# Row masks for the parts of eight running streams, and gate sums from token quarters

## The chip, the cores and the metric

The kernel runs on one core of a Trainium2 chip. The metric is the device time of one execution in microseconds (us). The core's engines are PE (TensorE, matrix products into PSUM), DVE (VectorE), ACT (ScalarE), POOL (GpSimd) and SP (which only starts DMAs here). Each engine takes its instructions in its own fixed order.

## The reference, cut to what matters

Two layers are applied to one prompt of 1024 tokens and to 8 running streams of 16 tokens each. The second layer, mixer B, is an mLSTM with 4 heads of width 512; only its two places below are changed.

```
gates = concat([q, k, v]) @ w_gates + b_gates          # 8 columns: 4 input gates, 4 forget gates
num   = (s @ v) + w_inter * (q @ C)                    # per token of a stream; C is 512x512
C_new = decay * C + k^T (w * v)                        # per head and per stream
h     = num / max(|den|, exp(-m_t))
```

For the running streams, `C` comes from outside: 4 heads x 8 streams = 32 matrices of 1 MB, each of which is read, multiplied by 16 queries (`q @ C`), updated and written back.

## The kernel before, in words

Tokens are held as 9 tiles of 128 (8 of the prompt, the ninth holds the 8 streams of 16), or as three thirds of 384. Activations lie with features on the partitions.

**Features.** Mixer B's input part runs over 16 blocks of 128 features (`Feature`). At the end of each, `gates` (L819) adds the block's share of the gates of all 1152 tokens into one PSUM tile `gp` (L721): one matmul for each third, weights `gsum` of 8 columns, each into its own column tile of TensorE (partitions 0, 32, 64). After the last block three copies (L905) bring `gp` to SBUF.

**z steps and streams.** Then 24 steps compute the z half of the projection (`z_to`), and the main loop runs over 32 units (head h, tile n of 128 prompt tokens). The 32 `Stream`s, in order of head and then of stream b = 0..7, ride in both: `open_stream` loads C into two tiles `c0`, `products` (L1130) is called one step or unit later, `finish` (L1152) after it. Streams 0 to 9 ride in the z steps, streams 10 to 31 with one unit each. I number them s0 to s31; each head has eight, so s7, s15, s23 and s31 are the last of their heads (b = 7).

`products` makes `q @ C` for 32 tokens, of which 16 belong to this stream: four matmuls `sm<-c,qT` of 32 columns, one for each quarter of the 512 features, side by side in the four column tiles; the four 32-row parts of the PSUM tile `pa` still have to be added. ACT copies `pa` to a tile `ev` (L1141). Then four matmuls on `sk` and four DVE operations (`c<-c,decB,sm`, L1148) update C.

`finish` does something when b is 3 or 7. A quad of four matmuls `sm<-ev,selm` adds the parts of four streams and puts the 16 useful rows of each into 32 rows of `po`; ACT copies the result and starts a store to `ni_d`. `rows_out` (L1324) reads it back when the unit of the ninth tile (a rider) is computed.

Other names in the rows: `x` (L1399) adds a projection to the residual, `raw<-sm,colB,sk` (L1380) is the skip gate, `dd` (L1230) the decay mask, which needs the loaded row `cw`, `bst` and `dn` (L1337, L1343) the head norm, `Cst` (L1297) the prompt's matrix memory, `Ch`/`Cl`, `va`, `s`, `q` the high and low parts of operands of three-pass products.

**What sets the order.** PE's order is the program's order (all its instructions pass through `Ordered`, so they all show L58). The order on the other engines is set when the kernel is built, by a scheduler that works with its own estimate of when each operand is ready; on the chip each engine keeps that order and waits where an operand is late. PSUM is eight buffers, all named `sm`, given out in rotation.

Of the kernel before, what the change touches and what calls it, by code (L numbers as in the profile page):

```python
# [8 lines left out]
F32 = mybir.dt.float32  # L9
F32R = mybir.dt.float32r  # L10
AF = mybir.ActivationFunctionType
# [59 lines left out]
def trunk_kernel(ctx: ExitStack, tc: tile.TileContext, ins: dict, outs: list):  # L71
# [57 lines left out]
    sk_d = [dram.tile([DH, NT * P], F32, name=f"sk_d{h}") for h in range(H)]  # L129
    z_d = [dram.tile([DH, NT * P], F32, name=f"z_d{h}") for h in range(H)]  # L130
    cw_d = dram.tile([H, 2, NT * P], F32, name="cw_d")
    ni_d = [dram.tile([2, P, DH], F32, name=f"ni_d{h}") for h in range(H)]
    x1_d = [dram.tile([P, D], F32, name=f"x1_d{n}") for n in range(NT)]
    st_d = [dram.tile([SB, 3 * SL, 2, DH], F32R, name=f"st_d{h}") for h in range(H)]

# [582 lines left out]
    gtok = const.tile([P, NT, 8], F32, name="gtok")  # L718
    G.memset(gtok, 0.0)

    gp = ps.tile([P, BT], F32, name="sm")  # L721
    cv0 = ins["state_mlstm_conv"][0].rearrange("b j e -> (b j) e")


    class Feature:
# [93 lines left out]
        def gates(self):  # L819

            f = self.f
            for b in range(NB):
                T.matmul(gp[32 * b:32 * b + 8], gsum[:, 0, f], self.xc[b], start=(f == 0), stop=(f == NF - 1), skip_group_check=True)

        def new_history(self):
            f = self.f
# [75 lines left out]
    gt = gt_stack.enter_context(tc.tile_pool(name="gt", bufs=1, side="right", reuse_waits="tile"))  # L902
    NTK = NT * P
    gsb = gt.tile([8, NTK], F32, name="rA")
    for b in range(NB):  # L905
        V.tensor_copy(out=gsb[:, b * BT:(b + 1) * BT], in_=gp[32 * b:32 * b + 8])
    z_to(4)


# [118 lines left out]
        T.transpose(tp[:, c * 32:(c + 1) * 32], n0t[:, c * P:(c + 1) * P], ident[:32, :32])  # L1028
    V.tensor_copy(out=n0T.rearrange("p c b h -> p (c b h)"), in_=tp[:, :P])

    selm = dw.tile([P, 2, 32], F32, name="selm")
    G.memset(selm, 0.0)
    for r0 in range(0, P, 32):
        for q in range(2):
            V.tensor_copy(out=selm[r0:r0 + 32, q, :SL], in_=ident[r0:r0 + 32, r0 + q * SL:r0 + (q + 1) * SL])

    def load_qkv(pool, h, n, want, prev=None, bufs=None):

# [80 lines left out]
    class Stream:  # L1119
# [12 lines left out]
        def products(self):  # L1132
            d, b = self.d, self.b
            pa = ps.tile([P, DH], F32, name="sm")

            b2 = slice(b // 2 * 32, b // 2 * 32 + 32)
            for c in range(DC):
                T.matmul(pa[32 * c:32 * c + 32], d.g["qT"][:, c, b2], self.c0[c // 2][:, c % 2], start=True, stop=True)
            ev = dw.tile([P, DH], F32, name="ev", bufs=4)
            d.ev.append(ev)  # L1140
            d.last = A.copy(out=ev, in_=pa)  # L1141
            for hf in range(2):
                c0 = self.c0[hf]
                for cc in range(2):
                    c = hf * 2 + cc
                    pc = ps.tile([P, DH], F32, name="sm")
                    T.matmul(pc, self.sk[:, 0, c * P:(c + 1) * P], self.sk[:, 1, :], start=True, stop=True)
                    V.scalar_tensor_tensor(out=c0[:, cc], in0=c0[:, cc], scalar=decB[:, d.h, 8 + b:9 + b], in1=pc,  # L1148
                                           op0=ALU.mult, op1=ALU.add)
                S.dma_start(out=C_s[0, b, d.h, hf * 256:(hf + 1) * 256].rearrange("(c p) e -> p c e", p=P), in_=c0)  # L1150

        def finish(self):  # L1152

            d, b = self.d, self.b
            if b % 4 == 3:
                po = ps.tile([P, DH], F32, name="sm")
                for i in range(4):
                    T.matmul(po[32 * i:32 * i + 32], selm[:, i % 2], d.ev[i], start=True, stop=True)
                d.ev = []
                ni = rawp.tile([P, DH], F32, name="raw")  # L1160
                A.copy(out=ni, in_=po)
                A.dma_start(out=ni_d[d.h][b // 4], in_=ni)

    heads = []
    streams = []
# [149 lines left out]
    def rows_out(u, a):  # L1315
# [5 lines left out]
        if u.smp:  # L1321
            if a == 0:
                u.ni = rawp.tile([P, DH], F32, name="raw")
                S.dma_start(out=u.ni, in_=ni_d[h].rearrange("a (b r) e -> (a b) r e", r=32)[:, :SL])  # L1324
            V.tensor_tensor(out=hn[:, a, :256], in0=num[:, :256], in1=u.ni[:, a * 256:(a + 1) * 256], op=ALU.add)
            if a == 0:
                V.tensor_tensor(out=hn[:, 0, 256:257], in0=num[:, 256:257], in1=dint[:, h:h + 1], op=ALU.add)
# [279 lines left out]
```

## Time and profile before

| what | value |
|---|---|
| time of the runs shown | 1933.91 us median of 3 (1932.88 to 1936.30) |
| profiled execution | 1929.5 us, span of the core 1927.8 us |
| granted TensorE clock | 0.996 |
| PE busy | 1887.7 us, 98% |
| DVE, ACT, POOL busy | 63%, 45%, 35% |
| features, from the first gate block to the last | 871.7 to 1138.0 us |
| quads `sm<-ev,selm` | 1272.8 to 1757.1 us |

The engine that sets the time is PE, so a change counts by what it does to PE: columns that it streams, gaps between two kinds of matmul, and waits. A timeline row groups instructions of one kind that follow each other; a record of a matmul includes its pipeline, so the next row can start before it ends. What a block costs is read from its start to the start of what follows it.

### The profile page before, as it was taken

Reading aid. Unit: us, or ns where it says so; the run is one execution under the profiler, and the core shown is the slowest. Engines: PE = TensorE matmul, PEld = TensorE weight load, DVE = VectorE, ACT = ScalarE, POOL = GpSimd, SP = SyncE. Lnnn points to the kernel's source line nnn. Section 1 sums busy time; section 2 is a strip of 40 time slices with the busy share of each in tenths; the row PEclk is TensorE's granted clock in tenths of the full one; section 3 lists DMA queues with packets and bytes.
Section 4 is the critical chain, followed back from the end, with each engine's and each line's share of the span. In section 5 each row is a group of like instructions: output and inputs, shape, how many; then the busy total and the mean of one; then the engine's idle time right before and its main releaser. Section 6 shows DMA issues by size and latency. Waiting matters only on the chain.

```text
span 1927.8 us, 32016 instructions
## 1 busy us (share of the span) xinstructions
PE 1887.7 (98%) x11553; PEld 1676.0 (87%) x11553; DVE 1216.1 (63%) x2406; ACT 862.4 (45%) x1760; POOL 674.9 (35%) x725
## 2 busy tenths in 40 slices
PE   7999999999999999999999999999999999999998
PEld 6888999999999778888999989888977887788887
DVE  5832567777776454567666655222388687688786
ACT  5422444444444343446655554222354444444564
POOL 2000234444442000024444421100167457457586
PEclk9999999999999999999999999999999999999999
DMA  6222343333334854435555564787898898876543
GB/s 217 93 93 73 96 109 100 100 98 99 101 97 122 263 152 143 131 92 157 152 160 166 164 186 124 240 256 247 263 320 267 263 287 273 262 239 196 153 130 125
DMA packets 345305, 328.20 MB, mean 170 GB/s; under 512 B 28164, under 2 KB 276436, under 8 KB 345148
## 3 DMA queue, kind: packets, MB, share of 16 engines
q1 hardware_dynamic: 278444, 255.72, 43.4%
q10 hardware_dynamic: 66512, 69.85, 11.7%
q8 instruction: 91, 1.49, 0.3%
q14 instruction: 66, 0.54, 0.1%
q0 software_dynamic: 192, 0.59, 0.1%
HBM read 203.07 MB, written 123.02 MB: 169 GB/s over the span
## 4 chain that ended last, share of the span: by engine, by line
PE 79%; DMA 7%; DVE 5%; POOL 3%; ACT 2%; issue 2%; ACTq 0%; SPq 0%; POOLq 0%; DVEq 0%
PE sm L58 79%; DMA cw<-cw_d 1%; POOL Cl L90 1%; DMA out<-c 1%; DMA z_d<-st 1%; DVE c L1148 1%; POOL va L90 1%; DMA kT<-k_d 1%; DMA vv<-vb_d 1%; DMA c<-in_state_mlstm_C 1%; DVE raw L1380 0%; DVE w L90 0%; DMA st_d<-w 0%; POOL q L90 0%; DVE Cst L1297 0%
## 5 line engine op out<-in xcount | busy, mean ns | idle before, releaser
L58 PE MATMUL sm<-xh,w 128*128 128x384 f32 x1536 | 410.4, 341 | 1.8 <-issue 1.2
L58 PEld LDWEIGHTS sm<-xh,w 128*128 128x128 f32 x1536 | 281.0, 188 | 10.0 <-issue 6.5
L58 PE MATMUL sm<-xl,w 128*128 128x384 f32 x768 | 260.1, 339 | 0.0
L58 PE MATMUL sm<-Xh,w 128*128 128x288 f32 x1024 | 216.9, 299 | 4.3 <-ACT c L499 4.3
L58 PE MATMUL sm<-w,o 128*128 128x512 f32 x864 | 209.7, 398 | 2.1 <-ACT o L89 1.2
L58 PE MATMUL sm<-w,os 128*128 128x512 f32 x864 | 200.3, 393 | 4.5 <-ACT os L89 3.5
L58 PEld LDWEIGHTS sm<-w,os 128*128 128x128 f32 x864 | 162.4, 189 | 40.8 <-ACT os L89 6.0
L58 PEld LDWEIGHTS sm<-w,o 128*128 128x128 f32 x864 | 160.0, 188 | 40.2 <-ACT o L89 1.4
L58 PE MATMUL sm<-w,Xh 128*128 128x512 f32 x576 | 180.5, 394 | 0.9 <-DVE w L90 0.9
L58 PEld LDWEIGHTS sm<-Xh,w 128*128 128x128 f32 x1024 | 168.9, 190 | 4.7 <-ACT c L499 4.5
L58 PE MATMUL sm<-S,w 128*128 128x288 f32 x1152 | 163.8, 297 | 0.0
L90 DVE TENSOR_TENSOR w<-r,w 128x512 fp32r<-128x512 f32 x176 | 137.9, 790 | 35.1 <-ACT w L89 34.4
L58 PEld LDWEIGHTS sm<-S,w 128*128 128x128 f32 x1152 | 155.1, 188 | 0.8
L90 POOL TENSOR_TENSOR Cl<-Cst,Ch 128x514 fp32r<-128x514 f32 x96 | 128.7, 1352 | 73.6 <-ACT Ch L89 50.3
L58 PE MATMUL sm<-Xl,w 128*128 128x288 f32 x512 | 151.9, 297 | 0.0
L58 PEld LDWEIGHTS sm<-xl,w 128*128 128x128 f32 x768 | 144.8, 189 | 0.0
L90 DVE TENSOR_TENSOR w<-raw,w 128x1024 fp32r<-128x1024 f32 x43 | 55.9, 1300 | 130.6 <-ACT w L89 126.6
L89 ACT CAST w<-r 128x512 fp32r<-128x512 f32 x176 | 107.2, 618 | 61.5 <-PE sm L58 29.1
L58 PEld LDWEIGHTS sm<-w,Xh 128*128 128x128 f32 x576 | 108.2, 190 | 24.0 <-DVE w L90 1.8
L58 PE MATMUL sm<-w,Xl 128*128 128x512 f32 x288 | 113.0, 392 | 0.0
L90 DVE TENSOR_TENSOR os<-or,os 128x384 fp32r<-128x384 f32 x96 | 52.8, 555 | 88.0 <-ACT os L89 87.8
L58 PE MATMUL sm<-va,k 128*128 128x258 f32 (+1 forms) x768 | 102.9, 284 | 0.5 <-DVE raw L1380 0.4
(310 smaller groups left out, 3643.5 us busy)
## 6 DMA issues: line engine op xcount, KB each, us to landing
c<-in_state_mlstm_C SPq DMA_DIRECT2D x64, 512.0 KB
out<-c SPq DMA_DIRECT2D x64, 512.0 KB
r<-in_a_w_in SPq DMA_DIRECT2D x96, 256.0 KB
or<-o_d SPq DMA_DIRECT2D x96, 192.0 KB
raw<-in_b_w_in SPq DMA_DIRECT2D x32, 512.0 KB
qT<-q_d SPq DMA_DIRECT2D x40, 256.0 KB
vh<-v_d SPq DMA_DIRECT2D x48, 192.0 KB
vb_d<-st ACTq DMA_DIRECT2D x48, 192.0 KB
```

Source lines behind the costliest of these rows:

```text
L58: ins = fn(*args, **kw)
L89: first = A.copy(out=hi, in_=src)
L90: (lo_eng or V).tensor_tensor(out=lo, in0=src, in1=f32(hi), op=ALU.subtract)
L1148: V.scalar_tensor_tensor(out=c0[:, cc], in0=c0[:, cc], scalar=decB[:, d.h, 8 + b:9 + b], in1=pc, op0=ALU.mult, op1=ALU.add)
```

## The change

Four edits.

1. `gates`: the 1152 tokens are put into four column tiles of 288 token columns each, in place of three of 384. As a block's `xc` still comes in thirds, the four quarters are made by six matmuls (288, 96, 192, 288, 192 and 96 columns). `gp` is cleared by DVE first, and four copies of 8x288 take it to SBUF.
2. `products`: two streams share one `ev` tile. Each stream's `pa` holds 32 rows for each quarter, of which alternate 16 rows are its own; the even stream's are kept by ACT with a scale of 1 or 0 for each row (`qsel[:, 0]`), the odd stream's are added by one DVE operation, `ev = pa * qsel[:, 1] + ev`.
3. `finish`: the quad is made only when b = 7, with the four shared tiles; `selm` is then a plain sum of the four quarters, and the result has all 128 rows of the head.
4. `ni_d` is one tile for each head, stored and read back in one piece; `selm` is made by 4 copies in place of 8, and `qsel` by one sum over `blk8`.

```
-    gp = ps.tile([P, BT], F32, name="sm")
+    gp = ps.tile([P, QT], F32, name="sm")
+    V.memset(gp, 0.0)
...
-            for b in range(NB):
-                T.matmul(gp[32 * b:32 * b + 8], gsum[:, 0, f], self.xc[b], start=(f == 0), stop=(f == NF - 1), skip_group_check=True)
+            for q, b, c0, c1, o in ((0, 0, 0, 288, 0), (1, 0, 288, 384, 0), (2, 1, 192, 384, 0), (3, 2, 96, 384, 0),
+                                    (1, 1, 0, 192, 96), (2, 2, 0, 96, 192)):
+                T.matmul(gp[32 * q:32 * q + 8, o:o + c1 - c0], gsum[:, 0, f], self.xc[b][:, c0:c1], start=(f == 0 and o == 0), stop=(f == NF - 1), skip_group_check=True)
...
+    selm = dw.tile([P, 32], F32, name="selm")
     for r0 in range(0, P, 32):
+        V.tensor_copy(out=selm[r0:r0 + 32], in_=ident[r0:r0 + 32, r0:r0 + 32])
+    qsel = dw.tile([P, 2], F32, name="qsel")
+    V.tensor_reduce(out=qsel, in_=blk8.rearrange("p (a q) -> p q a", q=2), axis=mybir.AxisListType.X, op=ALU.add)
...
-            ev = dw.tile([P, DH], F32, name="ev", bufs=4)
-            d.ev.append(ev)
-            d.last = A.copy(out=ev, in_=pa)
+            if b % 2 == 0:
+                ev = dw.tile([P, DH], F32, name="ev", bufs=4)
+                d.ev.append(ev)
+                d.last = A.activation(out=ev, in_=pa, func=AF.Copy, scale=qsel[:, 0:1])
+            else:
+                ev = d.ev[-1]
+                d.last = V.scalar_tensor_tensor(out=ev, in0=pa, scalar=qsel[:, 1:2], in1=ev, op0=ALU.mult, op1=ALU.add)
...
-            if b % 4 == 3:
+            if b == SB - 1:
                 po = ps.tile([P, DH], F32, name="sm")
                 for i in range(4):
-                    T.matmul(po[32 * i:32 * i + 32], selm[:, i % 2], d.ev[i], start=True, stop=True)
+                    T.matmul(po[32 * i:32 * i + 32], selm, d.ev[i], start=True, stop=True)
...
-                A.dma_start(out=ni_d[d.h][b // 4], in_=ni)
+                A.dma_start(out=ni_d[d.h], in_=ni)
```

On PE nothing but the gate blocks and the quads is different; of the eight quads those of s3, s11, s19 and s27 are gone. On DVE, 16 operations `ev<-sm,qsel,ev` are new. Where one of them stands is shown for s23, the last stream of the third head. DVE before, from the second half of the projection `x` of a unit to the update of C (c_16764 and c_16766 are the two tiles of C of s23):

```order
L1399 TENSOR_TENSOR x_3_14029<-x_3_14029,sm 128x512
L1230 TENSOR_TENSOR dd<-cw,m_pr 128x128
L1399 TENSOR_TENSOR x_3_14029<-x_3_14029,sm 128x512
L1380 SCALAR_TENSOR_TENSOR raw<-sm,colB,sk 128x128 x4
L1337 BN_STATS bst<-hn 128x6
L1343 SCALAR_TENSOR_TENSOR dn<-hn,tok 128x1
L1337 BN_STATS bst<-hn 128x6
L1148 SCALAR_TENSOR_TENSOR c_16764<-c_16764,decB,sm 128x512 x2
L1148 SCALAR_TENSOR_TENSOR c_16766<-c_16766,decB,sm 128x512 x2
```

DVE now, in the same place (most line numbers are 7 higher after the change):

```order
L1406 TENSOR_TENSOR x_3_14063<-x_3_14063,sm 128x512
L1237 TENSOR_TENSOR dd<-cw,m_pr 128x128
L1406 TENSOR_TENSOR x_3_14063<-x_3_14063,sm 128x512
L1387 SCALAR_TENSOR_TENSOR raw<-sm,colB,sk 128x128 x4
L1344 BN_STATS bst<-hn 128x6
L1350 SCALAR_TENSOR_TENSOR dn<-hn,tok 128x1
L1344 BN_STATS bst<-hn 128x6
L1148 SCALAR_TENSOR_TENSOR ev<-sm,qsel,ev 128x512
L1155 SCALAR_TENSOR_TENSOR c_16776<-c_16776,decB,sm 128x512 x2
L1155 SCALAR_TENSOR_TENSOR c_16778<-c_16778,decB,sm 128x512 x2
```

The `ev` operation stands behind the gate and three operations of the head norm. The same is true for s15; for s31 it stands one `bst` earlier.

The second place is s30 (an even stream, with no new DVE operation of its own). DVE before:

```order
L1348 SCALAR_TENSOR_TENSOR dn<-bmv,dn 128x1
L1230 TENSOR_TENSOR dd<-cw,m_pr 128x128
L1399 TENSOR_TENSOR x_2_14028<-x_2_14028,sm 128x512
L1325 TENSOR_TENSOR hn<-sm,raw 128x256
L1327 TENSOR_TENSOR hn<-sm,dint 128x1
L1325 TENSOR_TENSOR hn<-sm,raw 128x256
L1380 SCALAR_TENSOR_TENSOR raw<-sm,colB,sk 128x128 x4
L1337 BN_STATS bst<-hn 128x6
```

and now:

```order
L1406 TENSOR_TENSOR x_2_14062<-x_2_14062,sm 128x512 x2
L1332 TENSOR_TENSOR hn<-sm,raw 128x256
L1334 TENSOR_TENSOR hn<-sm,dint 128x1
L1332 TENSOR_TENSOR hn<-sm,raw 128x256
L1387 SCALAR_TENSOR_TENSOR raw<-sm,colB,sk 128x128 x4
L1237 TENSOR_TENSOR dd<-cw,m_pr 128x128
L1355 SCALAR_TENSOR_TENSOR dn<-bmv,dn 128x1
L1344 BN_STATS bst<-hn 128x6
```

The mask `dd` has moved from ahead of the second `x` to behind the four gate operations.

The third place is s19, whose quad is gone (c_15829 and c_15851 are its first tile of C before and now). DVE before, from its first update on:

```order
L1380 SCALAR_TENSOR_TENSOR raw<-sm,colB,sk 128x128 x4
L1148 SCALAR_TENSOR_TENSOR c_15829<-c_15829,decB,sm 128x512
L1382 TENSOR_TENSOR raw<-raw,zz 128x512
L1148 SCALAR_TENSOR_TENSOR c_15829<-c_15829,decB,sm 128x512
L1148 SCALAR_TENSOR_TENSOR c_15831<-c_15831,decB,sm 128x512 x2
L90 TENSOR_TENSOR w<-raw,w 128x1024
L90 TENSOR_TENSOR o_16013<-raw,o_16013 128x512
L1297 SCALAR_TENSOR_TENSOR Cst<-Cst,decB,sm 128x258
L1297 SCALAR_TENSOR_TENSOR Cst<-Cst,decB,sm 128x256
L90 TENSOR_TENSOR w<-raw,w 128x1024
L1337 BN_STATS bst<-hn 128x6
L1343 SCALAR_TENSOR_TENSOR dn<-hn,tok 128x1
```

and now:

```order
L1387 SCALAR_TENSOR_TENSOR raw<-sm,colB,sk 128x128 x4
L1148 SCALAR_TENSOR_TENSOR ev<-sm,qsel,ev 128x512
L1155 SCALAR_TENSOR_TENSOR c_15851<-c_15851,decB,sm 128x512
L1389 TENSOR_TENSOR raw<-raw,zz 128x512
L1155 SCALAR_TENSOR_TENSOR c_15851<-c_15851,decB,sm 128x512
L1155 SCALAR_TENSOR_TENSOR c_15853<-c_15853,decB,sm 128x512 x2
L90 TENSOR_TENSOR w<-raw,w 128x1024
L1304 SCALAR_TENSOR_TENSOR Cst<-Cst,decB,sm 128x258
L1304 SCALAR_TENSOR_TENSOR Cst<-Cst,decB,sm 128x256
L90 TENSOR_TENSOR o_16035<-raw,o_16035 128x512
L1344 BN_STATS bst<-hn 128x6
L1350 SCALAR_TENSOR_TENSOR dn<-hn,tok 128x1
```

One operation more stands ahead of everything from the first update of C on; `o` changes places with two `Cst`. Both lists go on to the third `Cst` (in the second list the second `w` comes between). s27 has the same order as s19.

## Rows read from the trace of the kernel before

**Rows 1.** The page: span, busy time of the engines, chain by engine.

```profile
span 1927.8 us, 32016 instructions
PE 1887.7 (98%) x11553; PEld 1676.0 (87%) x11553; DVE 1216.1 (63%) x2406; ACT 862.4 (45%) x1760; POOL 674.9 (35%) x725
PE 79%; DMA 7%; DVE 5%; POOL 3%; ACT 2%; issue 2%; ACTq 0%; SPq 0%; POOLq 0%; DVEq 0%
```

**Rows 2.** Stretches: length, busy PE, PEld, DVE, ACT, POOL, clock, DMA share, GB/s.

```profile
1225.00:1382.00 157.00, 156.19 (x886) 137.80 (x879) 43.58 (x57) 37.17 (x61) 7.65 (x5) 1.00 0.79 253
1382.00:1500.00 118.00, 115.52 (x772) 93.06 (x771) 89.21 (x197) 57.16 (x116) 72.45 (x66) 1.00 0.93 292
1625.00:1765.00 140.00, 137.75 (x907) 112.15 (x906) 110.76 (x240) 62.69 (x123) 79.44 (x72) 1.00 0.78 246
```

**Rows 3.** PE timeline at a gate block: start, length, ..., idle before and its releaser.

```profile
1009.57 0.83 PE L58 MATMUL sm<-xc,gsum 128*8 128x384 f32 x6
1010.33 0.29 PE L58 MATMUL sm<-ident,cl 128*27 128x128 f32 x1
```

**Rows 4.** ACT timeline ahead of the first gate block.

```profile
872.76 0.37 ACT L764 COPY xmp<-sm 128x256 f32<-128x256 f32 x1
873.34 0.55 ACT L779 ACTIVATE xc<-xc 128x384 f32<-128x384 f32 x1
```

**Rows 5.** PE timeline in the first gate block.

```profile
873.93 0.81 PE L58 MATMUL sm<-xc,gsum 128*8 128x384 f32 x2 [1.44 <-ACT xc L779]
```

**Rows 6.** PE timeline at the quad of s3, in the z steps.

```profile
1272.77 1.07 PE L58 MATMUL sm<-ev,selm 128*32 128x512 f32 x8
1273.77 0.44 PE L58 MATMUL sm<-xh,w 128*128 128x384 f32 x1
```

**Rows 7.** PE timeline at the quad of s11.

```profile
1402.67 1.06 PE L58 MATMUL sm<-ev,selm 128*32 128x512 f32 x6
1404.10 1.05 PE L58 MATMUL sm<-ev,selm 128*32 128x512 f32 x2 [0.37 <-ACT ev L1141]
1406.28 0.51 PE L58 MATMUL sm<-Ch,q 128*128 128x258 f32 x2 [0.34 <-POOL q L90]
```

**Rows 8.** Groups of DVE, 1382 to 1765 us: busy, mean ns, idle before.

```profile
L1148 DVE SCALAR_TENSOR_TENSOR c<-c,decB,sm 128x512 f32<-128x512 f32 x88 | 60.2, 735 | 0.5
```

**Rows 9.** DVE timeline at s23.

```profile
1615.55 0.29 DVE L1230 TENSOR_TENSOR dd<-cw,m_pr 128x128 f32<-128x128 f32 x1 [3.64 <-DMA cw<-cw_d]
...
1618.78 0.41 DVE L1337 BATCH_NORM_STATS2 bst<-hn 128x6 f32<-128x256 f32 x1
1619.11 2.04 DVE L1148 SCALAR_TENSOR_TENSOR c<-c,decB,sm 128x512 f32<-128x512 f32 x3
```

**Rows 10.** PE timeline at the quad of s23.

```profile
1617.52 1.07 PE L58 MATMUL sm<-ev,selm 128*32 128x512 f32 x8
1618.52 0.63 PE L58 MATMUL sm<-va,s 128*128 128x258 f32 x3
```

**Rows 11.** PE timeline at s15: ahead of its quad, and 8 us behind it.

```profile
1476.51 0.49 PE L58 MATMUL sm<-sk 48*128 48x512 f32 x1 [1.25 <-DVE x L1399]
...
1485.48 1.16 PE L58 MATMUL sm<-qT,kT 128*128 128x128 f32 x8 [0.20 <-DVE Cst L1297]
```

**Rows 12.** DVE timeline behind s19.

```profile
1544.78 0.29 DVE L1230 TENSOR_TENSOR dd<-cw,m_pr 128x128 f32<-128x128 f32 x1 [2.64 <-POOL q L90]
...
1554.68 0.47 DVE L1297 SCALAR_TENSOR_TENSOR Cst<-Cst,decB,sm 128x258 f32<-128x258 f32 x1
```

**Rows 13.** PE timeline at the quad of s19 and behind it.

```profile
1545.48 1.61 PE L58 MATMUL sm<-ev,selm 128*32 128x512 f32 x8
...
1555.20 1.66 PE L58 MATMUL sm<-w,o 128*128 128x512 f32 x6
```

**Rows 14.** DVE timeline at s30.

```profile
1736.78 1.36 DVE L1230 TENSOR_TENSOR dd<-cw,m_pr 128x128 f32<-128x128 f32 x1 [1.55 <-POOL va L90]
```

**Rows 15.** PE timeline at s30.

```profile
1738.79 0.49 PE L58 MATMUL sm<-sk 48*128 48x512 f32 x1 [1.68 <-DVE x L1399]
```

More of the change, by code (lines that the diff above doesn't have):

```diff
@@ L131, in trunk_kernel @@
     cw_d = dram.tile([H, 2, NT * P], F32, name="cw_d")
-    ni_d = [dram.tile([2, P, DH], F32, name=f"ni_d{h}") for h in range(H)]
+    ni_d = [dram.tile([P, DH], F32, name=f"ni_d{h}") for h in range(H)]
     x1_d = [dram.tile([P, D], F32, name=f"x1_d{n}") for n in range(NT)]
@@ L904, in trunk_kernel @@
     gsb = gt.tile([8, NTK], F32, name="rA")
-    for b in range(NB):
-        V.tensor_copy(out=gsb[:, b * BT:(b + 1) * BT], in_=gp[32 * b:32 * b + 8])
+    for q in range(4):
+        V.tensor_copy(out=gsb[:, quarter(q)], in_=gp[32 * q:32 * q + 8])
     z_to(4)
@@ L1029, in trunk_kernel @@
     V.tensor_copy(out=n0T.rearrange("p c b h -> p (c b h)"), in_=tp[:, :P])
-    selm = dw.tile([P, 2, 32], F32, name="selm")
-    G.memset(selm, 0.0)
+    selm = dw.tile([P, 32], F32, name="selm")
     for r0 in range(0, P, 32):
-        for q in range(2):
-            V.tensor_copy(out=selm[r0:r0 + 32, q, :SL], in_=ident[r0:r0 + 32, r0 + q * SL:r0 + (q + 1) * SL])
+        V.tensor_copy(out=selm[r0:r0 + 32], in_=ident[r0:r0 + 32, r0:r0 + 32])
+    qsel = dw.tile([P, 2], F32, name="qsel")
+    V.tensor_reduce(out=qsel, in_=blk8.rearrange("p (a q) -> p q a", q=2), axis=mybir.AxisListType.X, op=ALU.add)
     def load_qkv(pool, h, n, want, prev=None, bufs=None):
@@ L1323, in rows_out @@
                 u.ni = rawp.tile([P, DH], F32, name="raw")
-                S.dma_start(out=u.ni, in_=ni_d[h].rearrange("a (b r) e -> (a b) r e", r=32)[:, :SL])
+                S.dma_start(out=u.ni, in_=ni_d[h])
             V.tensor_tensor(out=hn[:, a, :256], in0=num[:, :256], in1=u.ni[:, a * 256:(a + 1) * 256], op=ALU.add)
```

## The prediction

> **What bounds the kernel now.** I read the page first [rows 1]: PE is busy for 1887.7 of 1927.8 us and carries 79% of the chain that ended last, so an edit counts by what PE gains or waits. Then I cut the span into stretches [rows 2]: in the z steps DVE is at 43.58 / 157 = 28%, in the main loop's stream part at 76 to 79%, and the DMA engines at 0.93 there at first. An engine at three quarters in the mean can be late at a given place, so I read the timelines of PE and DVE at each place that the change touches. Last I laid the new order of DVE beside these times, because the diff moves 16 evacuations of PSUM to an engine whose order is fixed.
>
> The profiled execution took 1929.5 us, 4.4 us less than the median of the runs shown, 1933.9. I work out a difference on its trace and add it to the median. About 0.2% (3.9 us) is what a measurement of this kernel can tell from no change.
>
> **Gate blocks.** Sixteen blocks of three matmuls, each of which shows as two records. The group starts at 1009.57 and what follows at 1010.33: 0.76 us [rows 3]. Six records of some 0.49 us lie in 0.83 us, so three run side by side and the second three follow them: two waves of about 0.33 us and 0.10 us around them. With 288 columns in a tile instead of 384 a wave is 0.33 x 0.75 = 0.25 us, the block 0.50 + 0.10 = 0.60, and I leave 0.02 for twice the matmuls: 0.14 us less, x 16 = -2.3 us. Bounds: -2.6 (no cost for the added matmuls) to +2.6 (rival 2).
>
> In the first block PE waits 1.44 us for ACT's `xc` [rows 5], which stood behind three copies that began at 872.76, while it began itself at 873.34 [rows 4]. ACT's new order has it ahead of them: up to 0.58 us, and I take -0.5, since DVE ends the input at about the time when the first copy began.
>
> The memset of `gp` and the fourth copy to SBUF are single DVE instructions on 288 columns at the ends of the feature part. Building `selm` has half the copies and one sum. I cost them at nothing: PE has projection work in its own order there. Bounds -0.5 to +0.5.
>
> A page's rule speaks against the smaller matmuls. The Trainium skill, "TensorE: Matmul & The Clock Gate", Part 3, Packing small matmuls, says that matmuls start and end strictly in the program's order. The two waves in 0.83 us [rows 3] have equal lengths and cannot show what a short one does behind a long one. By the rule this edit would cost time; that is rival 2.
>
> **Quads that go.** A quad without a wait takes 1618.52 - 1617.52 = 1.00 us [rows 10], at s3 1273.77 - 1272.77 = 1.00 as well [rows 6]; about 0.10 us of change between forms goes with it (the 0.10 around a gate block). Four of eight go: 4.4 us, if PE could use it.
>
> - s3: the z steps are PE work, DVE is at 28% [rows 2]: -1.1 us.
> - s11: PE stands 0.37 us for ACT's `ev`, and the second part of the quad ends only about 1405.1. But at 1406.28 PE waits for POOL's `q` [rows 7], which does not read `ev`; with the quad gone PE gets to the same wait earlier. I take 0, with -2.4 as the bound (the wait of PE, 1404.10 - 1402.67 = 1.43, and the quad's 1.0).
> - s19: DVE starts at 1544.78 [rows 12] and has no gap until the third `Cst`, which ends at 1554.68 + 0.47 = 1555.15, and PE goes on at 1555.20 [rows 13]. So the quad's 1.5 us is given back at that point. The new order has all the same operations ahead of this `Cst`, and `ev` as well. An STT (scalar_tensor_tensor) of this shape takes 735 ns, and back to back about 2.04 / 3 = 0.66 us after the first [rows 8, 9]. So PE goes on 0.7 us later: +0.7, bound -1.6 (the quad's record, if that wait is not what binds).
> - s27: the same order and the same price, +0.7.
>
> **Quads that stay.** They now hold eight streams, and the fourth matmul reads a tile that DVE writes last. At s23, DVE cannot begin before the load of `cw` lands: `dd` at 1615.55 after 3.64 us of idling. In the new order `ev` follows the second `bst`, where `c` began, at 1619.11 [rows 9]. It ends at 1619.11 + 0.74 = 1619.85. The quad begins at 1617.52 [rows 10]; three of its matmuls can run, the last waits. At s11 the quad shows what such a wait costs: the last pair started at 1404.10 and the following row about 1.0 us later. So the block is 1619.85 - 1617.52 + 1.0 = 3.3 us against 1.0: +2.35. Bounds: 0 (DVE gets there earlier by 2.3 us) and +3.0 (one operation more ahead of it). Behind this matmul on PE stands the whole numerator of the next unit, and nothing in PE's order can go round it.
>
> This pattern stands three times in the main loop. At s15 it is the same, but 8 us later PE waits 0.20 us for `Cst` [rows 11], which then is covered: +2.1. At s31 `ev` is one `bst` earlier, 1619.11 - 1618.78 = 0.33 [rows 9]: +2.0. At s7 the quad is a z step after the products: 0.
>
> On the rule that both engines should empty PSUM: the Trainium skill, "TensorEngine Tiling (Array Packing)", PSUM Bottleneck, advises to use ScalarE and VectorE together. Here the trace differs in the place: ACT is at 45% and DVE at 63% [rows 1], and 79% in the stretch, so the move loads the fuller engine. By that rule the move would gain; by the rows it is where the three waits come from.
>
> **Other odd streams.** Eleven of the sixteen new DVE operations are in the main loop: five are named above; of s13, s17, s21, s25 and s29, with 0.66 us of DVE each, I take +0.4 in all, since DVE has idle time there [rows 2]. Bounds 0 and 5 x 0.7 = +3.3.
>
> **s30.** PE waits 1.68 us for `x` [rows 15], which stood behind `dd`, and `dd` stood behind a gap of 1.55 us and took 1.36 [rows 14]. In the new order `dd` comes after both `x` and after the gate: the wait goes, -1.7 (bounds -1.7 and 0: something else of that unit may be late by then).
>
> **Other engines.** ACT loses 16 + 4 evacuations; it is at about half its time, and PE waits for it at one quad only: nothing, beyond s11. Four stores of 256 KB go. In the stretch with a DMA share of 0.93 at 292 GB/s [rows 2] one is 0.9 us of transfer, and the `cw` loads that DVE waits for might land that much sooner: taken as 0, bound -0.9 at each of the three. SP's loads for a new head wait for the evacuation of the stream before, which can now be DVE's and some 2 us later; SP holds the loads behind it for as long. A head opens three units ahead of its use: 0.
>
> **Sum.** -2.3 - 0.5 - 1.1 + 0 + 0.7 + 0.7 + 2.35 + 2.1 + 2.0 + 0.4 - 1.7 = +2.65 us. On the trace 1927.8 becomes 1930.4; on the median 1933.9 + 2.6 = **1936.5 us**.
>
> **Rivals.**
>
> 1. *The waits do not come* (faster). If the `cw` loads land some 2.5 us sooner against PE, DVE is ready at the three quads, and PE's wait of 1.25 us at s15 [rows 11] goes too. For it: the DMA engines are the reason for DVE's start at these places, and four stores go. Against: PE itself needs `x`, which is right behind `dd` on DVE, so a later `cw` holds both, and the operations between `x` and `ev` take 3.4 us whenever they start. Sum without the three: -2.3 - 0.5 - 1.1 - 1.7 + 1.4 + 0.4 - 1.4 = -5.2: 1928.7 us.
> 2. *Strict order within a gate block* (slower). By a mechanism in which a short matmul holds its tile until a longer one ahead of it has ended, the two parts of a quarter add up as 288 + 192 = 480 columns: two waves of 0.33 x 480 / 384 = 0.41, a block of 0.92 us, +0.16 x 16 = +2.6 instead of -2.3. Total +7.5: 1941.4 us. Decided by whether the block is above 0.76 us. For it the rule above; against, that records of different tiles start side by side [rows 3].
> 3. *DVE is the bound of every unit with an odd stream* (slower). It holds if the gap-free run behind s19 [rows 12] is the rule: then each of the five others costs 0.66 too (+3.3 in place of +0.4), and s30 gives nothing back, since DVE would be late by as much. Total +2.65 + 2.9 + 1.7 = +7.2: 1941.2 us. Decided where PE's waits for DVE in 1382 to 1765 us, now few, show up in streams beside the named ones. For it: DVE at 79%; against: DVE's gaps in front of `dd`, 3.64 us at s23.
> 4. *Nothing binds*: the quads' time and the waits cancel in slack that I did not see: 1933.9 us.
>
> **How the numbers follow.** Forecast 0.47, rival 1 0.20, rival 2 0.10, rival 3 0.15, rival 4 0.08. The forecast's own range is -1.5 to +6 (s11 or s19 gaining part of a quad; waits at the upper bound), 1932.4 to 1940. Of its 0.47 I count 0.32 within 0.2% and 0.15 above, as its middle is 1.2 us below the limit. Rival 1 gives 0.18 faster and 0.02 within; rivals 2 and 3 0.22 slower and 0.03 within; rival 4 0.08 within. So faster 0.18, the same 0.45, slower 0.37. The range reaches down to rival 1's, 1929, and up to rival 3's, 1941.5.
>
> **What the changed profile would show.** Gate blocks at about 0.62 us from start to the next row; at the quads of s15, s23 and s31 a PE wait for DVE `ev` of some 1.9 to 2.4 us with the last two records apart from the first six; PE at the third `Cst` behind s19 and s27 waiting for it by 2 us or more; no wait of PE at s30's last `sk`; the first gate block's wait below 1 us. It is wrong if PE's waits for `ev` add up to less than 3 us, if gate blocks are longer than before, or if PE keeps the quad's time behind s19.

## The result and the profile after

The changed kernel took 1947.81 us (median of 4 runs, 1945.16 to 1950.91), the kernel before 1933.39 beside it: a ratio of 1.0088 [1.0066, 1.0110], slower by about 17 us, or by 14.4 us between the medians. The forecast was 1936.5, and its range ended at 1941.5.

The page of the profiled execution (1947.13 us): span, busy time of the engines, chain by engine.

```profile
span 1945.4 us, 32125 instructions
PE 1892.3 (97%) x11617; PEld 1686.9 (87%) x11617; DVE 1226.4 (63%) x2421; ACT 852.8 (44%) x1740; POOL 677.4 (35%) x724
PE 79%; DVE 7%; DMA 6%; POOL 3%; ACT 2%; issue 2%; SPq 0%; ACTq 0%; POOLq 0%; DVEq 0%
```

Against [rows 1], PE has four quads less to do and yet is busy for 4.6 us longer, and it is idle for 1945.4 - 1892.3 = 53.1 us in place of 40.1. So two things need a cause: 13 us of new waiting, and matmuls that took longer. The seven largest sums of what PE waited for from 838 us on (total, times, longest):

```profile
PE sm L58 <- DVE ev L1148: 3.6, 3, 1.3
PE sm L58 <- DVE Cst L1304: 3.3, 2, 2.4
PE sm L58 <- ACT raw L1103: 3.1, 1, 3.1
PE sm L58 <- POOL s L90: 3.1, 3, 1.9
PE sm L58 <- POOL q L90: 2.2, 5, 0.6
PE sm L58 <- DVE x L1406: 1.9, 3, 1.2
PE sm L58 <- DVE xl L90: 1.4, 1, 1.4
```

The wait for `ev` was forecast. Those for `Cst`, `raw`, `s` and `xl` are almost all new, and the forecast has no term for most of them. Laid against the trace before, start by start of the same PE instruction, the difference builds up so (us):

| place | forecast | measured |
|---|---|---|
| to 838, code that is the same in both | 0 | +3.1 |
| 838 to 874: `xl` late, and a clock dip | 0 | +3.2 |
| gate blocks (the first -2.2, one more -1.2) | -2.8 | -5.2 |
| 1219: first normaliser, `raw` late | 0 | +4.7 |
| s3, quad gone | -1.1 | -1.2 |
| 1396: start of the main loop, `q` late | 0 | +2.6 |
| s11, quad gone, then `s` late, and a clock dip | 0 | +1.9 |
| s15 | +2.1 | +0.1 |
| s19, quad gone | +0.7 | -0.3 |
| 1574: unit of s20, `s` and `q` late | 0 | +2.4 |
| s23 | +2.35 | +2.3 |
| s27, quad gone, then `Cst` late | +0.7 | +1.7 |
| s30 | -1.7 | -2.4 |
| s31 | +2.0 | +2.0 |
| all other places | +0.4 | +3.0 |
| sum | +2.65 | +17.9 |

The terms that were seen are mostly near their forecast; the rows with a forecast of 0 hold most of the miss. The trace before was a quick run of its kernel (1929.5 us), which is part of the +3.1 at the top. Two entries are not the work of the change. The -1.2 at one gate block (992 us) is -1.0 in e2 and in e12 too, which have the gates of before. The dip at 841 us stands behind the same two gaps of PE, 1.18 and 0.6 us, that the trace before has there without a dip; e12 and e13, whose code is that of before up to there, show it as well.

**What came as forecast.** A gate block, PE timeline (start, length, idle before and its releaser in brackets):

```profile
1011.68 0.67 PE L58 MATMUL sm<-xc,gsum 128*8 128x288 f32 x12
1012.28 0.29 PE L58 MATMUL sm<-ident,cl 128*27 128x128 f32 x1
```

0.60 us where [rows 3] had 0.76, to the hundredth what two waves of 288 columns give. The kept quad of s23, first PE, then DVE:

```profile
1631.15 1.06 PE L58 MATMUL sm<-ev,selm 128*32 128x512 f32 x6
1633.53 1.05 PE L58 MATMUL sm<-ev,selm 128*32 128x512 f32 x2 [1.32 <-DVE ev L1148]
```

```profile
1629.19 0.29 DVE L1237 TENSOR_TENSOR dd<-cw,m_pr 128x128 f32<-128x128 f32 x1 [3.63 <-DMA cw<-cw_d]
...
1632.41 0.41 DVE L1344 BATCH_NORM_STATS2 bst<-hn 128x6 f32<-128x256 f32 x1
1632.74 0.73 DVE L1148 SCALAR_TENSOR_TENSOR ev<-sm,qsel,ev 128x512 f32<-128x512 f32 x1
```

DVE still starts behind the load of `cw` (3.63 us, as in [rows 9]); `ev` ends at 1633.47 and the last pair of the quad starts 0.06 us later. PE's wait is 1.3 us where 1.9 to 2.4 were forecast, since three of the four matmuls run meanwhile; but from the quad to the next row it is 3.35 us, and the forecast was 3.3. And s30, where PE had waited 1.68 us [rows 15]:

```profile
1753.90 1.20 PE L58 MATMUL sm<-sk 48*128 48x512 f32 x4
1755.02 0.62 PE L58 MATMUL sm<-va,s 128*128 128x258 f32 x3
```

No wait is left ahead of the fourth `sk`.

**What was not forecast.** At 861 us, ahead of the first gate block:

```profile
861.25 0.45 PE L58 MATMUL sm<-xh,w 128*128 128x384 f32 x1 [1.41 <-DVE xl L90]
```

At the first normaliser, in the z steps, PE and then ACT:

```profile
1219.27 1.19 PE L58 MATMUL sm<-raw,blk 128*8 128x512 f32 x2 [3.11 <-ACT raw L1103]
...
1220.87 0.53 PE L58 MATMUL sm<-xl,w 128*128 128x384 f32 x1
...
1223.61 0.34 PE L58 MATMUL sm<-xl,w 128*128 128x384 f32 x1
```

```profile
1217.12 0.62 ACT L89 CAST va<-vv 128x512 fp32r<-128x512 f32 x1 [5.08 <-DMA vv<-vb_d]
...
1218.53 0.69 ACT L1103 ACTIVATE raw<-sm,tok 128x512 f32<-128x512 f32 x1 [0.40 <-ACT st L879]
```

ACT's own order puts the cast of a loaded `vv` ahead of `raw`. That load is late, ACT stands 5.08 us, and PE, which needs `raw`, 3.11. Three such casts stand ahead of `raw` in the kernel before too; there ACT waits 0.25 us at the third. PE is not early here: it comes to this matmul 1.1 us later than before. What is late is the third load of `vv`, on SP, and it waits for the first `va<-vv,va` on POOL to be done with the first `vv`. Before:

```profile
1203.21 1.19 POOL L90 TENSOR_TENSOR va<-vv,va 128x512 fp32r<-128x512 f32 x1 [4.00 <-ACT va L89]
```

```profile
1204.43 0.45 SPq L1050 DMA_DIRECT2D vv<-vb_d  x1
```

Now:

```profile
1206.91 1.81 POOL L90 TENSOR_TENSOR w<-raw,w 128x512 fp32r<-128x512 f32 x1 [6.73 <-ACT w L89]
1208.69 1.18 POOL L90 TENSOR_TENSOR va<-vv,va 128x512 fp32r<-128x512 f32 x1
```

```profile
1210.36 8.98 SPq L1052 DMA_DIRECT2D vv<-vb_d  x3
```

On ACT and on POOL the first `va` has changed places with `w<-raw`, and the third load starts 5.9 us later. It is the same in e1 (1211.36), which has the gate edit alone; in e2, with the gates of before, `va` comes first and the load starts at 1208.17.

Behind the wait the same `xl` matmul takes 0.53 us and then 0.34: the clock is low until shortly before 1223.6. The same shows at the start of the main loop and behind s11:

```profile
1396.75 0.97 PE L58 MATMUL sm<-va,q 128*128 128x258 f32 x3 [1.09 <-ACT q L89]
...
1411.84 0.58 PE L58 MATMUL sm<-va,s 128*128 128x258 f32 x1 [1.86 <-POOL s L90]
...
1413.09 0.80 PE L58 MATMUL sm<-Ch,q 128*128 128x258 f32 x2 [0.23 <-POOL q L90]
...
1574.80 0.44 PE L58 MATMUL sm<-va,s 128*128 128x258 f32 x1 [0.93 <-POOL s L90]
...
1711.38 6.92 PE L58 MATMUL sm<-w,o 128*128 128x512 f32 x22 [2.40 <-DVE Cst L1304]
```

(the fourth row is in the unit of s20, the last behind s27). At s20 it is again an order that has changed, that of POOL. Before:

```profile
1559.33 3.79 POOL L90 TENSOR_TENSOR Cl<-Cst,Ch 128x514 fp32r<-128x514 f32 x3
1563.07 0.46 POOL L90 TENSOR_TENSOR s<-dd,s 128x128 fp32r<-128x128 f32 x1
```

and now:

```profile
1570.11 1.28 POOL L90 TENSOR_TENSOR w<-raw,w 128x512 fp32r<-128x512 f32 x1
1571.35 2.54 POOL L90 TENSOR_TENSOR Cl<-Cst,Ch 128x514 fp32r<-128x514 f32 x2
1573.85 0.90 POOL L90 TENSOR_TENSOR s<-dd,s 128x128 fp32r<-128x128 f32 x1
```

A `w<-raw,w` that stood behind `s` is ahead of it. `s` starts 10.8 us later than before, PE's work in this unit 9.8. At s11 POOL's order up to `s` is the old one.

Stretches of 10 us around these places, with the granted clock ahead of the DMA share and GB/s:

```profile
1215.00:1225.00 10.00, 6.89 (x27) 5.54 (x26) 0.25 (x1) 3.65 (x6) 2.44 (x2) 0.83 0.58 180
1395.00:1405.00 10.00, 8.87 (x57) 8.43 (x57) 5.49 (x17) 6.87 (x17) 2.88 (x4) 0.83 0.89 285
1410.00:1420.00 10.00, 7.93 (x42) 7.63 (x43) 6.74 (x13) 2.14 (x5) 4.27 (x4) 0.66 1.02 286
1574.00:1584.00 10.00, 8.83 (x61) 8.53 (x62) 7.25 (x19) 3.62 (x8) 3.83 (x5) 0.83 0.90 293
1708.00:1718.00 10.00, 7.60 (x31) 6.05 (x31) 8.20 (x17) 4.32 (x8) 8.69 (x7) 0.83 0.72 236
```

The kernel before shows 1.00 in each of these. A mean of 0.83 is some 3.4 us at 0.5, which is 1.2 GHz, and the rest at 2.4.

### The profile page after: what moved, and what is told of

The parts are those of the page before. It is cut to its first block, busy times and chain, and to the rows that moved or that the text cites. A ratio compares the mean times of both kernels' runs of the same rounds, so it can differ in the third digit from the quotient of the medians.

```text
span 1945.4 us, 32125 instructions
## 1 busy us (share of the span) xinstructions
PE 1892.3 (97%) x11617; PEld 1686.9 (87%) x11617; DVE 1226.4 (63%) x2421; ACT 852.8 (44%) x1740; POOL 677.4 (35%) x724
## 4 chain that ended last, share of the span: by engine, by line
PE 79%; DVE 7%; DMA 6%; POOL 3%; ACT 2%; issue 2%; SPq 0%; ACTq 0%; POOLq 0%; DVEq 0%
PE sm L58 79%; DMA cw<-cw_d 2%; POOL Cl L90 1%; DVE c L1155 1%; DMA st_d<-w 1%; DMA vv<-vb_d 1%; DVE w L90 1%; DMA out<-c 1%; POOL va L90 1%; DVE Cst L1304 1%; DMA x<-in_x_prompt 1%; DVE raw L1387 1%; DMA vh<-v_d 0%; DVE dn L1350 0%; DMA kT<-k_d 0%
```

## The experiments

A ratio is to the kernel before on the same chip; 0.001 is 1.93 us. Theory names are those of the texts on record.

**One part at a time.** e1 is the kernel before with the edit of the gates alone (`gp`, its memset, `gates`, the four copies).

> The kernel before with the gate edit alone (six matmuls in four column tiles, the memset, four copies). Theory A: the edit is two things. The sixteen gate blocks fall from 0.76 to about 0.6 us and PE's waits in them shrink: 5 us less between the first and the last block. But the new order on SP and ACT that comes with this edit puts a third cast va<-vv, with a load behind it, ahead of the first head's keys raw<-sm,tok: PE waits about 3 us at the first sm<-raw,blk and the granted clock falls to 0.5 behind it, together +4.5 us. Net about -1 us on the median of before, 1932 to 1933. Rival B (the loss lies in the quads' edit alone): no such wait at the first sm<-raw,blk, 1928 us. Rival C (the 6 us that the changed kernel loses ahead of the first gate block belong to the edit): 1938 us.

Measured: 1933.66 us, 1.0015 [1.0000, 1.0030]. The gate edit alone brings no time, it costs up to 6 us. (That a third cast comes ahead of the keys is not new, as the rows above show; its load comes later.) The blocks do get shorter, but PE waits 2.4 us for `xl`, 2.7 for `raw` and 1.7 for the load of `sk`.

e2 is the changed kernel with the gates of before.

> The changed kernel with the gates as before: row masks, one quad of sums per head, DVE adding the odd streams. Theory A: no wait at the first sm<-raw,blk; PE waits for DVE ev of 1.9 to 2.6 us at the quads of s15, s23 and s31, waits for POOL s at the units of s11 and s20 and for Cst behind s27, with some 3 us at half the granted clock behind each of the longer waits: about +12 us on before, 1945 us. Rival B' (the three ev waits alone, the other waits are accidents of the order that came with the gates): +2 to +4 us, 1936 us.

1941.83 us, 1.0048 [1.0030, 1.0065], +9.3: the `ev` waits are the same, `xl` and `raw` do not wait.

e8 is the changed kernel without the sixteen additions on DVE (it leaves the odd streams' parts out of the result):

```
-            else:
-                ev = d.ev[-1]
-                d.last = V.scalar_tensor_tensor(out=ev, in0=pa, ...)
```

> The changed kernel without the 16 DVE operations that add the odd streams: their parts are left out of the sums. Theory A: the three waits for DVE ev go (6.9 us), and the Cst waits behind s19 and s27 shrink by 0.7 us each: 8 us less than the changed kernel, 1940 us. Rival H (the waits for POOL s and Cst come from the quads that left, not from the added DVE work): only the ev waits go, 7 us or less; rival D (DVE is not what the quads wait for): no gain.

1939.34 us, 1.0034 [1.0020, 1.0048]. So the additions cost 10.4 us by the ratios, 8.5 by the medians. What is left waits elsewhere:

```profile
PE sm L58 <- DVE Cst L1301: 5.0, 4, 2.0
PE sm L58 <- POOL s L90: 3.8, 2, 3.1
PE sm L58 <- POOL q L90: 3.0, 5, 0.8
```

The `Cst` waits are longer with less on DVE ahead of them: there PE comes sooner, and not DVE later.

e17 is e8 with the gates of before: four quads gone, no operation added. e18 puts four matmuls without use where the quads stood:

```
+            if b == 3:
+                fill = ps.tile([P, DH], F32, name="sm")
+                for i in range(4):
+                    T.matmul(fill[32 * i:32 * i + 32], selm, d.ev[0], start=True, stop=True)
```

> The gates as before, four quads gone, and none of the 16 DVE additions: the parts of the odd streams are left out. So what is left of the change is less work on PE (4 us), ACT (20 evacuations less) and the DMA queues (four stores less), and nothing added on any engine. Theory P (the gains of the forecast do not come because PE only gets sooner to waits that other engines set, and the granted clock falls behind them): 0 to 4 us more than before, 1931 to 1935 us, with waits for POOL s or q behind s11 and s20 and for Cst behind s27. Rival Q (the quads' time is a gain and the rest of the loss came with the gates): 3 to 5 us less than before, 1927 us.

> The same with four idle matmuls where each removed quad stood, so that PE has as many blocks as before; nobody reads them. Theory P: not slower than the run without them, or 1 to 2 us faster by the clock: 1930 to 1934 us, and no stretch at half the clock behind s11 and s27. Rival Q: 4 us more than the run without them.

e17: 1933.84, 1.0012 [0.9999, 1.0024]. Four microseconds of PE work are gone, and nothing is gained. e18: 1941.39, 1.0048 [1.0033, 1.0064], 7.5 us more than e17. "Not slower" was wrong, and by the times Rival Q is no better: e17 is not below the kernel before. PE's waits from 838 us on, in the traces of e17 and then of e18:

```profile
PE sm L58 <- DVE Cst L1299: 4.8, 4, 1.8
```

```profile
PE sm L58 <- DVE Cst L1303: 0.8, 3, 0.4
```

Before, they were 0.2 us. With work in the quads' place the waits for `Cst` shrink by 4.0. Start by start, e17 gains 1.0 to 1.2 us on e18 at each place of a quad and gives it back at the next wait: behind s3 PE waits 0.96 us for `q` against 0.08, at s11 3.07 for `s` against 2.11, behind s19 1.83 for `Cst` against 0.19, behind s27 1.75 against 0.19. These two traces show that a quad's time comes back as a wait. The times do not: the trace of e18 is its shortest run and that of e17 its second longest, so the 7.5 us between the medians stay unexplained.

Against the kernel before, e8, e17 and e18 are not clean. The loads of a new head hang on the operation that they leave out (`d.last`) and start sooner: the third head's `cw` at 1399.72 in e17, at 1408.91 before. POOL's order follows, and at s11 `qT<-qT,cw` (1.72 us in e17), which stood behind `s`, is ahead of it. In e18, where PE has the work of before, it still waits 2.11 us for `s` at s11 and 1.49 at s20; the kernel before has no wait for `s`. So part of what these three runs lose is an order and not the quads.

**Taking single waits away.** e3 calls `finish` in the main loop one unit later, ahead of the next products:

```
+        for st in late:
+            st.finish()
...
-        for st in sts:
-            st.finish()
+        late = sts
```

> The changed kernel with every quad of the main loop one unit later on PE, just ahead of the next stream's products. Theory A: the three PE waits for DVE ev (2.34, 2.59 and 1.93 us) go, all else stays: 7 us less than the changed kernel, 1941 us. Rival D (DVE is the bound there: PE only gets to the next Cst or x sooner and waits there): no gain, 1946 to 1948 us.

1942.79, 1.0057 [1.0042, 1.0073], 5 us less than the changed kernel, 7 were expected. PE's waits for `ev` fall from 3.6 to 0.2 us, and the version still loses to the kernel before.

e5 clears `gp` at the first gate block (`if f == 0: V.memset(gp, 0.0)`) and not at its allocation.

> The changed kernel with the memset of gp, and so the first use of its PSUM buffer, moved from the start of the feature part to the first gate block. Theory A: all kernels with the gate edit lost 1.8 to 3.1 us at the second feature's last projection, waiting for DVE xl, and the one without it lost nothing there, because gp holds one of eight PSUM buffers some 45 us earlier; now that wait goes, 2 us less than the changed kernel, 1945 to 1946 us. Rival F (the wait comes from the order on DVE and not from the buffer): it stays.

1949.06, 1.0087 [1.0065, 1.0110]. The wait of 1.41 us at 861 us is gone, so the place of the memset made it, and PE is 1.7 us sooner behind it. But at the first gate block PE waits for `xc` and is 1.7 us later again, and the time is the same.

e4 moves the first normaliser from z step 15 to 16.

> The changed kernel with the first head's normaliser (the matmul sm<-raw,blk) one z step later; nothing else moves. Theory A: the wait of 3.1 us for ACT raw and the stretch at a granted clock of 0.5 behind it both go: 4.4 us less than the changed kernel, 1943.4 us. Rival E (the same lateness holds up something else, the load of sk<-st_d ahead of the first products): the wait only moves there, 1947 us.

1950.45, 1.0089 [1.0060, 1.0117]. The wait for `raw` goes; this one comes:

```profile
PE sm L58 <- DMA sk<-st_d: 6.0, 1, 6.0
```

The theory (a step more covers it) is wrong. ACT stands 6.45 us for the `vv` load here, and `sk` is read from `st_d`, which is stored from `raw`, so the wait moves along the chain.

e6 lets the loads of units 2 to 4 follow the first head's scaled keys, e9 those of units 1 to 4 and `sk` and `zz` of unit 0 (e9's lines):

```
-        u.g.update(load_qkv(ld, u.h, u.n, want, bufs=...))
+        prev = heads[0].scaled if u in units[:5] and (...) else None
+        u.g.update(load_qkv(ld, u.h, u.n, want, prev, bufs=...))
```

> The changed kernel with one constraint on the order: the loads for units 2 to 4 come behind the ACT operation raw<-sm,tok of the first head's keys, and with them the third cast va<-vv. Theory A: it is the order of these two that makes PE wait about 3 us at the first sm<-raw,blk (or, in the run with the later normaliser, 6 us for sk<-st_d); both go, with the stretch at half the granted clock: 4 to 5 us less than the changed kernel, 1943 us. Rival E2 (the DMA engines are late there whatever the order): the wait stays above 1.5 us, 1946 to 1948 us.

> The changed kernel with the main loop's first loads (units 1 to 4, and sk and zz of unit 0; none is used before 1380 us) put behind the ACT operation raw<-sm,tok of the first head's keys. The run that moved only the third cast still waited 2.3 us there, behind a store z_d<-st that took 5.7 us to land. Theory A2: it is these loads, which the gate edit's order lets in sooner, that hold up the z stores, the keys and st_d: the waits at the first sm<-raw,blk and sk<-st_d both fall below 0.5 us and the granted clock stays at 1.0 there: 4 to 6 us less than the changed kernel, 1942 to 1944 us. Rival E3 (the keys are late by something else): the two waits together stay above 3 us, 1947 to 1950 us.

e6: 1951.72, 1.0095 [1.0068, 1.0122]; `raw` still waits 2.3 us, since ACT stood 5.81 us for a store of `z_d`. e9: 1947.00, 1.0089 [1.0070, 1.0108]; the wait for `raw` is gone, that for `sk` is 2.8. No gain.

e10 is e1 with the later memset and e9's loads; e11 is e3 with both; e12 is the kernel before with e9's loads.

> The gate edit alone, with the memset of gp at the first gate block and the first loads of the main loop behind the first head's keys: the quads as before. Theory A2: with both side effects taken away the shorter gate blocks show: 3 to 6 us less than before, 1926 to 1929 us, against 1933.7 us for the gate edit alone. Rival I (the blocks' gain is given back at the next thing that PE waits for, the loads of C): within 2 us of before, 1930 to 1933 us.

> The changed kernel with three edits: late quads in the main loop, the memset of gp at the first gate block, and the first loads of the main loop behind the first head's keys. Theory A2: the three gains add up (5, 0 to 2 and 4 to 6 us): 1934 to 1938 us, still above before, as the waits for POOL s, q and Cst that stand where the quads were, and the clock behind them, remain. Rival J (the quads' edit is a gain once its waits are out of the way): below 1929 us.

> The kernel before with the same constraint on the first loads of the main loop and no other edit; it tells what the constraint is worth by itself. Theory A2: PE waits 0.8 us for sk<-st_d in the kernel before and not for the keys, so at most 1 us less than before: 1930 to 1932 us. Rival K (the constraint is a gain on any kernel, and not a repair of what the gate edit did): 3 us or more less than before, below 1928 us.

e10: 1936.41, 1.0026 [1.0014, 1.0039]. From 838 to 1140 us PE gains 3.0 us on the kernel before. Its largest waits are these:

```profile
PE sm L58 <- DVE x L1403: 5.6, 3, 2.4
PE sm L58 <- DMA sk<-st_d: 2.5, 1, 2.5
```

e11: 1941.65, 1.0063 [1.0043, 1.0082]; e12: 1933.15, 1.0014 [1.0001, 1.0027]. The loads alone cost at most some 5 us, and no mix of repairs reaches the kernel before.

e15 is e10 with the usual loads and the normaliser and first streams one z step later; e16 is the kernel before with that step (`first, rate = 16, ...`).

> The gate edit alone with the memset at the first gate block, and the first streams and the first normaliser one z step later, so that PE has other work while st_d and the keys are on their way. Theory N: the wait for sk<-st_d and the clock behind it go, the gain of the gate blocks is kept: 3 us less than before, 1928 us. Rival I: what is gained there is given back at the main loop's start: 1931 to 1934 us.

> The kernel before with its first streams and the first normaliser one z step later, the control of the run with the gate edit. Theory N: the wait of 0.8 us for sk<-st_d goes and nothing else: 0 to 1 us less than before, 1930 to 1931 us. Rival O (the streams' loads then collide with the main loop's first loads): 2 us or more above before.

e15: 1941.11, 1.0044 [1.0022, 1.0066]; e16: 1937.35, 1.0035 [1.0020, 1.0050]. Theory N is wrong in both. The step is itself a loss, so e15 says little on the gates.

**The clock.** e13 puts six holes on PE into z steps of the kernel before, each a matmul that waits for a chain of ACT copies of growing length:

```
+                    T.matmul(pt[:, :32], ident, hole[0], start=True, stop=True)
+                    A.copy(out=hole[0], in_=pt[:, :32])
+                    for j in range(k):
+                        A.copy(out=hole[0], in_=hole[0])
```

> The kernel before with six holes for PE in the z steps 24, 27, 30, 33, 36 and 39: at each a small matmul waits for a chain of 2, 3, 4, 5, 7 and 11 small ACT copies that starts from PE itself (some 1 to 5 us), in a stretch where no other engine is late. Theory C (the clock): a short hole costs its length; behind holes of about 2 us and more the granted clock is 0.5 for some 3 us and the following matmuls take twice as long, 1.2 to 1.7 us more than the hole at each. The holes together some 16 us, the sum 20 to 24 us more than before. Rival L (a hole costs its length and no more): 16 us, clock 1.0 behind all of them.

1955.95, 1.0131 [1.0111, 1.0150], +24.9 us. PE's waits at the holes, and the clock around one that ended at 1312.4:

```profile
PE sm L58 <- ACT hole L888: 14.7, 6, 4.9
```

```profile
1311.00:1313.00 2.00, 0.57 (x3) 0.51 (x3) 1.21 (x1) 1.32 (x4) 0.00 (x0) 0.50 0.74 280
1313.00:1315.00 2.00, 2.00 (x4) 0.30 (x4) 0.10 (x2) 0.18 (x1) 0.00 (x0) 0.50 0.95 277
1315.00:1317.00 2.00, 2.00 (x9) 2.00 (x10) 0.65 (x1) 0.00 (x0) 0.00 (x0) 0.69 0.73 273
```

The shortest hole (1.05 us of waiting, 1.6 us lost in all) leaves the clock up. At each of the other five (1.30 us of waiting and more) it falls to 0.50, so the 2 us of Theory C were too much, and the matmuls behind lose 1.5 to 1.6 us beside the wait. That is the price of a dip.

e7 is the changed kernel with the idle quads shown above; e14 adds 14 idle matmuls ahead of the first `sm<-raw,blk` and 6 ahead of the second unit's numerator.

> The changed kernel with four idle matmuls put back where the removed quads stood (behind s3, s11, s19 and s27); they read one finished tile and nobody reads them. Theory A: behind s11, s19 and s27 PE waits anyway, so the idle matmuls cost only at s3 (1 us), and where they fill a wait they keep the granted clock from falling to 0.5 behind it (at s11 some 1.7 us): 0 to 2 us less than the changed kernel, 1945 to 1948 us. Rival G (removing quads did gain their time and the loss is elsewhere): 4 us more than the changed kernel, 1952 us.

> The changed kernel with idle matmuls at six places: where the quads of s3, s11, s19 and s27 stood, ahead of the first sm<-raw,blk (14 of 128 columns), and ahead of the numerator of the main loop's second unit (6). Nobody reads them. Theory C: they fill PE's waits, so PE is not late by them, and the granted clock stays at 1.0 where it fell to 0.5: 3 to 5 us less than the changed kernel, 1943 to 1945 us, with more PE work than it. Rival M (the clock is a symptom, PE is bound by the waits' ends): as the changed kernel, 1947 to 1949 us; if the waits are not what binds, 6 us more.

e7: 1945.98, 1.0069 [1.0045, 1.0093]; e14: 1946.92, 1.0076 [1.0056, 1.0096]. Neither is measurably different from the changed kernel (1.0088). Behind the units of s20 and s27, e7 is 2.9 and 3.5 us ahead of the changed kernel, with more work on PE. The trace of e14 shows a clock of 0.996 and no dip behind 1200 us, and it was its shortest run (1940.81); the median of its clock is 0.993, against 0.990 of the changed kernel, and its time is only 0.9 us shorter by the medians, 2.3 by the ratios. So idle work takes dips and waits away, and on the whole it costs as much as it saves. The profiled execution of before had the same clock, 0.996, and took 1929.5: 11 us stand between the two without any dip in the main loop, idle work included.

## Why the prediction was wrong, point by point

**The step that failed** is the sum: it counts as gained time what PE no longer does ("Gate blocks ... -2.3", "-0.5", "s3 ... -1.1", "s30 ... -1.7") and costs the small edits at nothing ("PE has projection work in its own order there"). It laid the new order of DVE beside the trace, but at these places not those of ACT, POOL and SP, which the edits change too. Without the sixteen additions the forecast would have been -2.3 - 0.5 - 1.1 - 1.7 = -5.6; e8 measures +6.6 [+3.9, +9.3]. That is 12 of the 14 us between forecast and measurement, as far as e8's own order (see there) allows.

- *Gate blocks.* The size was right, 0.60 us, and rival 2 is refuted. The Trainium skill, "TensorE: Matmul & The Clock Gate", Part 3, Packing small matmuls, says that matmuls start and end in the program's order; with parts of 288, 96 and 192 columns the block took what two waves of 288 take, so that rule did not cost anything here. Yet the edit as a whole costs 2.9 us in e1 and 5.0 in e10. At the first normaliser the cause is the order of ACT and POOL that came with it: a load starts 5.9 us later, `raw` is late and then `sk`, whatever PE has gained.
- *Memset at nothing.* It costs a wait of 1.41 us at 861 us; with that removed (e5), as much comes back at the first gate block.
- *Quads that go.* At s3 PE gained 1.2 us as forecast. At the start of the main loop it waits 1.09 for `q`, with a dip behind; but e10, e13 and e16, which keep the quad of s3, wait 1.1 there too, so this is not shown to be the quad's doing. At s11 the forecast said that PE "gets to the same wait earlier". It does, and at that wait for `q` it is where it was, +0.0; the dip behind adds 1.9. At s19 and s27 `Cst` binds as forecast. At s27 PE waits 2.40 us and goes on 1.1 later than before, where 0.7 was forecast; without the DVE operation (e17) the wait is 1.75, so that operation's price was right, and the dip is what was missed. At s19 the wait is 0.91 and PE goes on 0.3 sooner.
- *POOL at s20.* No term. The wait for `s` and the dip behind it, +2.4, come from POOL's new order.
- *The additions.* Forecast 2.35 + 2.1 + 2.0 + 0.7 + 0.7 + 0.4 = 8.25, measured 8.5 to 10.4 (e8), and 7.0 with the gates of before (1.0048 against 1.0012). In the trace of e8 the kept quads at s15, s23 and s31 start what follows 2.36, 1.58 and 2.03 us sooner than in the changed kernel. At s15 the trace gives the gain of a vanished wait for `x` back with it: -1.4 + 2.3 - 0.8 = +0.1. This half was right in mechanism and about right in size. The five other odd streams of the main loop (s13 to s29) cost 0.3 us together, where 0.4 was forecast, which refutes rival 3 (it is two even ones, s14 and s22, that lose 0.9 and 1.3, in "all other places"). Rival 1, that `cw` lands sooner, did not come: DVE's wait was 3.63 us, before 3.64.
- *s30.* The wait went, as forecast (-2.4), but that is in part luck. With `dd` in its old place the wait is 2.4 us in e10, 0.2 in e1 and none in e12 and e16: it comes and goes between executions, and the forecast took it from one.
- *What was missing altogether.* Behind some of its waits PE runs at 1.2 GHz for some microseconds. e13 gives 1.5 to 1.6 us for each; the changed kernel has five such places between 1200 us and the end of the streams, the profiled execution of before none. By the medians of all runs the granted clock is 0.990 against 0.993, which is 0.003 x 1945 = 5.8 us: my estimate, from above, of what the clock takes of the loss, as PE would have to be busy in all of it. At one and the same clock, 0.991, the kernel before took 1932 to 1944 us, median 1937 (5 runs), and the changed one 1945.2 and 1950.9. The rest I put down to the waits themselves.

**Open.** Where the loads were moved out of the way (e6, e9, e10), ACT stands 5.8 to 6.5 us for a store of `z_d` in place of `vv`, before 2.94: why that store lands so late is not shown. No run keeps the old order on ACT, POOL and SP with the new work, so what the orders cost and what the waits cost that come with less work on PE are told apart at single places only, not in the total. The median of e18 is not explained. No version that was run beats the kernel before.

## What to carry to other kernels

Where one engine is busy for 98%, work taken off it is worth something only up to the next operand that another engine or a DMA delivers: before counting a gain, find that operand and its lead. An operation added to another engine ahead of such an operand costs its full time, and this can be read from the timeline to some tenths of a microsecond. Even a small edit can give every engine another order, so lay the new order of each engine, and not only of the one that gets more work, beside the times. A wait in one trace may be missing in the next execution, so look whether it stands in several. A new wait on PE can cost a dip of the clock beside its own length, here 1.5 to 1.6 us.

## What the runs showed of the hardware that was not expected

- A wait need not be long for a dip. The rows at 1574 us have one behind 0.93 us of waiting for `s`, that at 1396.75 one behind 1.09, while the hole of 1.05 us in e13 has none. Nor is the length enough to tell: in the profiled execution of before the waits of 1.44 us [rows 5] and 1.68 us [rows 15] have no dip behind them. The Trainium skill, "TensorE: Matmul & The Clock Gate", "Why this matters for your kernels", warns of long gaps between bursts of matmuls; the wait of 3.11 us agrees, and the dips behind the short ones go beyond it.
- The mean granted clock differs between executions of one program: 0.989 to 0.996 over the 92 runs of the kernel before that stood beside these experiments, the higher the shorter (about 1932 us at 0.992, 1927 at 0.996). The two traces that I compared were at 0.996 and 0.988, so a part of any difference between just two traces is this.
